# PSUM banks of the output pass, sigmoid's table, wo products in pairs and small closing products in a hybrid decoder layer

## The chip, the cores and the metric

The kernel runs on one core of a Trainium2 chip. The metric is the device time of one execution in microseconds (us). The kernel before took 1947.63 us, the median of three executions (1947.04, 1947.63, 1947.76). The engines are called PE (TensorE, matrix products; PEld is its loading of weights), DVE (VectorE), ACT (ScalarE), POOL (GpSimd) and SP (SyncE, which here only issues DMAs).

## The reference

One layer on 1024 tokens with 16 learned meta tokens ahead of them, width 1024, all in float32:

```
h = h + 1/2 * SwiGLU_1(RMSNorm(h))                 # d_ff 2816
u = RMSNorm(h) @ W_in                              # one projection for both groups
o = concat[ HGRN2(u_hgrn), StickBreaking(u_sb) ]   # 4 heads of 128; 8 heads of 64
h = h + o @ W_out
h = h + 1/2 * SwiGLU_2(RMSNorm(h))
```

`swiglu(h, w_in, w_out)` is `(silu(g) * u) @ w_out` with `g, u = split(h @ w_in)`. HGRN2 is a gated linear recurrence, computed in chunks of 128 tokens; its forget gate f is a sigmoid, its query and output gate pass through silu. Stick-breaking attention normalises q and k for each head (a root), and weights each earlier token by a sigmoid times a product of (1 - sigmoid). The output is h without the 16 meta tokens.

## The kernel before, in words

Float32 products are made of three products of rounded parts (hi x hi, lo x hi, hi x lo), each a 128x128 weight block by up to 512 columns. PE's instructions are issued in the order in which the program writes them; the other engines are scheduled by the compiler's queue order with a few forced orders (`issue_after`). The work runs in stages.

**First SwiGLU (from the start to about 690 us).** Each of its two matrix products is done by a Strassen-like scheme with seven block products. The input pass (`fast_in`; `quad`, `gate`, `up` inside it, L452 to L571) goes through the columns in quads. A quad opens four sums in PSUM, tagged qa, qb, qc and qd, of two banks each, in the pool `pin1`. Its results are gated on ACT (`gate`) and multiplied on DVE (`up`, L542 and L545), and stored as activations in DRAM. Tags of this pool get their banks in the order of their first use. The first use of any is `warm` (L843 to L847), 30 transposes of the identity ahead of the first data, in two tiles of tag qb. The sums of the meta tokens (`begin` with the products mq of L1014, and `finish`, L985 to L996, with the transpose mf) use the tag qd. Two other small groups of products are named later: mps (L901), transposes of the meta tokens, and nps (L262), sums for a norm with a 128x128 block of ones as weights and one column.

The output pass (`fast_out`, L619 to L745) uses the pool `pout1`, which takes over the same banks once `pin1` is closed. It opens four tiles y0 to y3 for its first step (A12 by B21), and x0 to x3 for its second; the meta tokens have a sum of their own there, tag m. For its first three q (blocks of 256 rows of w_out) it gathers the 36 products and issues them together, hi x hi of all first. Weights are halved into hi on ACT and lo on DVE (L652), eight slots in `self.parts["w"]`, and the activations in `self.parts["t"]`.

**Projections and stick-breaking attention (about 690 to 1146 us).** A projection of 128 columns (`project`, `hgrn_fill`, L1116 to L1195; products L249 to L251, tag proj, two banks) is done in pieces of 256 or 512 tokens. For column kind v the sum is copied (L1148) and stored (hg_v, L1150). For kind f, ACT makes two sigmoids (L1154, L1155) and DVE scales them (L1156, L1159); the results lie in `st` tiles, of which there are four. The first f columns follow the last step of `sb_qk` (L1464 to L1503), which normalises q and k of a pair of heads: DVE transposes, ACT squares and takes the root of the mean (L1488), DVE the reciprocal, POOL multiplies (L1492), DVE transposes back (L1498), and `put_split` (L1429, L1430) scales and splits on ACT and DVE and stores. It is done for p = 0 to 3. Where ACT goes over from the root to the sigmoid, the trace has a table load (ACT_TABLE_LOAD). `sb_v` splits v (L1450, L1451) and stores it with four DMAs on SP (L1458).

**HGRN2's recurrence with the first half of o @ W_out (about 1146 to 1263 us).** `weave` (L1741 to L1783) merges the steps of several generators: three lanes of heads (heads 0 then 3, head 1, head 2) and a "fill", `first_half_of_o`. It keeps a clock in declared durations, and starts a fill step whenever the fill's share of the work lies behind or no head is ready. A head's steps are known by their products: lvl (L1248, L1283), flip (L1508), knp (L1319), s and up (the state, L1327 and L1334, followed by four DVE operations L1337), op (L1347, L1351), onp (L1367). A fill step is one k of one sum of `mix_out`: three products named wo, 650 declared; 64 of them in all. The inputs oT are loaded from DRAM by SP.

**Second half, second SwiGLU, end.** The second SwiGLU has the same two passes; its output pass writes the result by rows. Its last step (A22) evicts x0 to x3 on DVE (L699) and stores them by SP (L705). The y sums are left earlier, while the steps after S4 run. After that only the program's closing drains follow (L2406).

Of the kernel before, what the change touches and what calls it, by code (L numbers as in the profile page):

```python
# [11 lines left out]
F32 = mybir.dt.float32  # L12
# [3 lines left out]
AF = mybir.ActivationFunctionType  # L16
# [4 lines left out]
P = 128  # L21
# [28 lines left out]
class Block:  # L50
# [742 lines left out]
    def open_tokens(self, ops, opened, prepare, rows_at, ev, operands):  # L793
# [9 lines left out]
        nc, x = self.nc, self.a["x"][0]  # L803
# [37 lines left out]
        ra = rows_in(0)  # L841
        nc.sync.dma_start(*self.loads.pop(0))
        for _ in range(2):  # L843
            warm = self.pin.tile([P, 512], F32, tag="qb", name="warm", bufs=2)
            for i in range(15):
                t = warm[:, P * (i % 4) : P * (i % 4) + P]
                nc.tensor.transpose(t, self.ident, self.ident)  # L847
# [616 lines left out]
    def sb_qk(self, p, qT, kT, pool, mix, dst):  # L1464

        nc = self.nc  # L1470
        ss, other = (
            pool.tile([P, 65], F32, tag=x, name=x, bufs=2) for x in ("sbs", "sbo")
        )
        nat = pool.tile([P, 65, 32], F32, tag="nat", name="nat", bufs=2)
        rows = [(qT, 0, 0, 16), (qT, 512, 16, 16), (kT, 0, 32, 16), (kT, 512, 48, 17)]
        for src, c0, b0, nb in rows:
            y = nat[:, b0 : b0 + nb]
            nc.vector.transpose(y.rearrange("p b d -> p (b d)"), src[:, c0 : c0 + 32 * nb])
            sq = pool.tile([P, 17, 32], F32, tag="sq4", name="sq4", bufs=2)[:, :nb]
            nc.scalar.activation(sq, y, AF.Square)  # L1480
            nc.vector.tensor_reduce(ss[:, b0 : b0 + nb], sq, mybir.AxisListType.X, ALU.add)
            yield 0, 1500
        for b in range(4):
            nc.scalar.copy(
                other[32 * b : 32 * b + 32], ss[32 * (b ^ 1) : 32 * (b ^ 1) + 32]
            )
        nc.vector.tensor_add(ss, ss, other)
        nc.scalar.activation(ss, ss, AF.Sqrt, bias=self.eps, scale=1.0 / 64)  # L1488
        nc.vector.reciprocal(ss, ss)
        for _, _, b0, nb in rows:  # L1490
            y = nat[:, b0 : b0 + nb]
            nc.gpsimd.tensor_mul(  # L1492
                y, y, ss[:, b0 : b0 + nb].unsqueeze(2).broadcast_to([P, nb, 32])
            )
        yield 0, 6000
        for src, c0, b0, nb in rows:
            t = src[:, c0 : c0 + 32 * nb]
            nc.vector.transpose(t, nat[:, b0 : b0 + nb].rearrange("p b d -> p (b d)"))  # L1498
            n = min(32 * nb, (SEQ if src is qT else T) - c0)
            gain, to = (self.qg8, dst[0]) if src is qT else (self.kg, dst[1])  # L1500
            with self.tc.issue_after(self.rounds[self.columns[-1]]) if p == 3 else ExitStack():
                self.put_split(to, p, slice(c0, c0 + n), t[:, :n], mix, gain)
            yield 0, 1500  # L1503
# [287 lines left out]
    def run(self):  # L1791
        nc, tc, a = self.nc, self.tc, self.a
# [20 lines left out]
        with ExitStack() as c0:  # L1813
            with ExitStack() as c1:
# [116 lines left out]
                with tc.manual_schedule(engines={nc.tensor.engine}), ExitStack() as c2:  # L1931
# [9 lines left out]
                    self.op = self.pool("op1", ctx=op_ctx)  # L1941
                    pout_ctx = ExitStack()
                    self.pout = self.pool("pout1", 1, PSUM, pout_ctx)
                    hT = ph.tile([P, KT, T], F32, name="hT")
                    self.ring_bufs, self.act_bufs, self.apart = 7, 5, True
                    early_w, hat = [], []
# [127 lines left out]
                    def between(step, q):  # L2074
                        if (step, q) in loads:
                            m, c = loads[step, q]
                            with tc.issue_after(self.last_act.ins):
                                nc.sync.dma_start(hT[:, m, c : c + n], xD[m, :, c : c + n])
                        if (step, q) == ("S2", 5):
                            nc.sync.dma_start(  # L2080
                                hT[:, :, :META], xD[:, :, :META].rearrange("k p t -> p k t")
                            )
                        if step == "S3" and 6 <= q < 10:
                            if q == 6:
                                norms[1] = norm_steps(
                                    c_b, lambda: [(self.pout, "y0"), (self.pout, "y1")], v, 2, 4
                                )
                            next(norms[1])
                        elif step == "A22":
                            if q == 0:  # L2090
                                norms[2] = norm_steps(
                                    c_a, lambda: [(self.pn, "nps")] * 2, v, 0, 1
                                )
                            for _ in range(2):
                                next(norms[1], None)
                            if 6 <= q < 10:
                                next(norms[2])
                            if q in (1, 3, 5):
                                early_w.append(self.col_tile(
                                    a["w_in"][0], {1: 2560, 3: 3072, 5: 2048}[q]  # L2100
                                ))
# [83 lines left out]
                with tc.manual_schedule(engines={nc.tensor.engine}):  # L2185
# [7 lines left out]
                    with ExitStack() as c2:  # L2193
                        self.att.append(self.pool("att1", ctx=c2))
                        tag = self.proj_tags[0]
# [11 lines left out]
                    for i, n in enumerate(LEVELS[:5]):  # L2207
                        m = self.masks[:, i, :].rearrange("p (b h r) -> p b h r", h=2, r=n)
# [33 lines left out]
            with tc.manual_schedule(engines={nc.tensor.engine}), ExitStack() as cx:  # L2242
                with ExitStack() as c1:
# [8 lines left out]
                    def from_dram(half):  # L2252
                        got = [[], []]
                        for k in range(4):
                            for i in range(2):
                                t = self.pool_o.tile([P, 512], F32R, tag="o", name="oT", bufs=16)
                                with tc.issue_after(self.last_load.ins) if half else ExitStack():
                                    self.last_oT = nc.sync.dma_start(
                                        t.bitcast(F32), oD[k, :, i, 512 * half : 512 * half + 512]
                                    )  # L2260
                                got[i].append(t)
                        return [Blocks(x) for x in got]

                    def first_half_of_o():
                        ws = {0: self.rows_tile(4, 0)}
                        o = [from_dram(0)]
                        for store in self.stores:
                            with tc.issue_after(self.last_oT.ins):
                                store()
                        yield 4000.0  # L2270
                        plan = [(m, half) for half in range(2) for m in range(KT)]
                        steps = self.mix_out(4, plan, o, ws, hD, hT, mix)
                        for i, (t, f) in enumerate(steps):
                            if i == 16:
                                o.append(from_dram(1))
                            f()
                            yield t

                    with ExitStack() as c2:
                        c2.push(hg_ctx)  # L2280
# [33 lines left out]
                    for i in summed(1, cB):  # L2314
                        if i == 4:
                            r = self.inv_rms_rows(sums[0], n, px, pps)
                        if i == 7:
                            r = self.spread_rows(r, n, px, pps)
# [36 lines left out]
                r = self.inv_rms_rows(sums[1], n, px, ppb)  # L2355
# [8 lines left out]
            with tc.manual_schedule(engines={nc.tensor.engine}), ExitStack() as c1:  # L2364
                self.ring = self.pool("ring", ctx=c1, side="right")
                hR = self.pool("h3", ctx=c1).tile([P, SEQ // P, D], F32, name="hR")
                self.op = self.pool("op", ctx=c1)
                self.pout = self.pool("pout2", 1, PSUM, c1)

                loads = {("A12", 2 * m): (m, 0) for m in range(4)}  # L2370
                loads.update({("A11", m): (4 + m % 4, 1 - m // 4) for m in range(8)})
                loads.update({("S2", m): (m, 1) for m in range(4)})

                def between(step, q):
                    if (step, q) in loads:
                        r, i = loads[step, q]
                        nc.sync.dma_start(
                            hR[:, r, 512 * i : 512 * i + 512],
                            h2R[P * r : P * r + P, 512 * i : 512 * i + 512],
                        )  # L2380

                self.ring_bufs, self.act_bufs, self.apart = 6, 6, False
                self.fast_out(
                    hR, (cA, cB), n, a["ffn2_w_out"][0], actD, lambda step: None, between, rows=True
                )


NAMES = [
# [21 lines left out]
```

## Time and profile before

| | |
|---|---|
| median of three executions | 1947.63 us |
| the profiled execution | 1946.68 us |
| span of its profile | 1944.9 us |
| PE busy | 1919.0 us (99%) |
| DVE busy | 1392.1 us (72%) |
| ACT busy | 848.6 us (44%) |
| granted PE clock, mean | 1.0 |
| HBM traffic over the span | 182 GB/s |

In the rows of a timeline the first number is the start in us from the start of the span, the second the time to the end of the last of the operations that the row groups (xcount), then engine, source line and operation, out<-in by tile names with partitions x elements; in brackets stands how long the engine had been idle before it, and what released it. In the rows by line stand the busy time of the group and the mean in ns, and behind the second bar the idle time before its instructions. In a window's row stand its bounds, its length, then for PE, PEld, DVE, ACT and POOL the busy time and the count, then the granted PE clock, the DMA engines' busy share and GB/s. A line with a q behind the engine's name (SPq) is of that engine's queue of instructions. Consecutive products of PE overlap, so a product's duration is longer than the distance to the next one's start.

### The profile page before, as it was taken

Reading aid. Unit: us, or ns where it says so; the run is one execution under the profiler, and the core shown is the slowest. Engines: PE = TensorE matmul, PEld = TensorE weight load, DVE = VectorE, ACT = ScalarE, POOL = GpSimd, SP = SyncE. Lnnn points to the kernel's source line nnn. Section 1 sums busy time; section 2 is a strip of 40 time slices with the busy share of each in tenths; the row PEclk is TensorE's granted clock in tenths of the full one; section 3 lists DMA queues with packets and bytes.
Section 4 is the critical chain, followed back from the end, with each engine's and each line's share of the span. In section 5 each row is a group of like instructions: output and inputs, shape, how many; then the busy total and the mean of one; then the engine's idle time right before and its main releaser. Section 6 shows DMA issues by size and latency. Waiting matters only on the chain.

```text
span 1944.9 us, 30254 instructions
## 1 busy us (share of the span) xinstructions
PE 1919.0 (99%) x10637; PEld 1619.7 (83%) x10637; DVE 1392.1 (72%) x2184; ACT 848.6 (44%) x1711; POOL 450.3 (23%) x625
## 2 busy tenths in 40 slices
PE   9999999999999999999999999999999999999999
PEld 7888888887888888889898978888888888888887
DVE  7977778877678665467777766667577767767774
ACT  7522343334444444366666635533223332344443
POOL 2010101001000003133333342210554544530000
PEclk9999999999999999999999999999999999999999
DMA  7265897758965325865453178656544444469473
GB/s 219 89 178 165 254 287 244 244 184 294 372 230 188 120 58 146 190 172 148 134 155 116 58 251 245 154 202 200 180 119 141 130 125 131 130 248 323 143 233 114
DMA packets 381687, 355.54 MB, mean 183 GB/s; under 512 B 129040, under 2 KB 284560, under 8 KB 381536
## 3 DMA queue, kind: packets, MB, share of 16 engines
q1 hardware_dynamic: 360768, 288.98, 49.2%
q0 software_dynamic: 20768, 64.63, 9.5%
q8 instruction: 84, 1.38, 0.3%
q14 instruction: 67, 0.55, 0.1%
HBM read 237.95 MB, written 115.57 MB: 182 GB/s over the span
## 4 chain that ended last, share of the span: by engine, by line
PE 90%; DVE 4%; DMA 2%; ACT 2%; issue 1%; POOL 0%; SPq 0%; DVEq 0%; ACTq 0%; POOLq 0%
PE o L735 22%; PE qb L452 18%; PE qa L452 12%; PE qc L452 12%; PE proj L249 5%; PE proj L251 5%; PE proj L250 5%; PE flip L1508 2%; PE wo L250 1%; PE wo L251 1%; PE wo L249 1%; PE mq L1014 1%; PE oacc L1587 1%; PE oacc L1585 1%; PE z L1657 1%
## 5 line engine op out<-in xcount | busy, mean ns | idle before, releaser
L452 PE MATMUL qb<-T,wh 128*128 128x512 f32 x1056 | 343.7, 390 | 0.4 <-DVE u L484 0.4
L452 PEld LDWEIGHTS qb<-T,wh 128*128 128x128 f32 x1056 | 198.2, 188 | 44.5 <-issue 3.3
L452 PE MATMUL qa<-B,wh 128*128 128x512 f32 x696 | 227.6, 392 | 0.3 <-ACT B L838 0.2
L249 PE MATMUL proj<-xh,wh 128*128 128x512 f32 (+2 forms) x640 | 212.4, 332 | 3.0 <-ACT st L1155 1.4
L362 DVE TENSOR_TENSOR wl<-s,wh 128x512 fp32r<-128x512 f32 x160 | 165.7, 1036 | 69.3 <-ACT wh L360 68.5
L735 PE MATMUL o<-t,w 128*128 128x512 f32 x924 | 211.8, 390 | 1.1 <-DVE u L545 1.1
L251 PE MATMUL proj<-xl,wh 128*128 128x512 f32 (+2 forms) x640 | 209.3, 327 | 0.8 <-DVE xl L1973 0.8
L735 PE MATMUL o<-parts 128*128 128x512 f32 x924 | 209.6, 389 | 0.0
L250 PE MATMUL proj<-xh,wl 128*128 128x512 f32 (+2 forms) x640 | 208.9, 326 | 0.0
L452 PE MATMUL qb<-T,wl 128*128 128x512 f32 x528 | 205.5, 389 | 0.0
L735 PEld LDWEIGHTS o<-t,w 128*128 128x128 f32 x924 | 172.8, 188 | 38.2 <-ACT sgm L994 1.5
L735 PEld LDWEIGHTS o<-parts 128*128 128x128 f32 x924 | 173.4, 188 | 36.0
L360 ACT CAST wh<-s 128x512 fp32r<-128x512 f32 x160 | 99.4, 622 | 185.6 <-PE qb L452 139.4
L452 PEld LDWEIGHTS qa<-B,wh 128*128 128x128 f32 x696 | 130.5, 188 | 29.3 <-issue 1.4
L360 ACT CAST wh<-raw 128x512 fp32r<-128x512 f32 x120 | 74.3, 621 | 143.7 <-PE qc L452 93.0
L452 PE MATMUL qa<-B,wl 128*128 128x512 f32 x348 | 135.5, 389 | 0.0
L249 PEld LDWEIGHTS proj<-xh,wh 128*128 128x128 f32 x640 | 120.9, 189 | 14.3 <-ACT st L1155 2.2
L251 PEld LDWEIGHTS proj<-xl,wh 128*128 128x128 f32 x640 | 120.9, 189 | 11.8 <-DVE xl L1973 1.2
L250 PEld LDWEIGHTS proj<-xh,wl 128*128 128x128 f32 x640 | 121.1, 189 | 9.1
L452 PEld LDWEIGHTS qb<-T,wl 128*128 128x128 f32 x528 | 99.1, 188 | 20.3
L452 PE MATMUL qc<-T,wh 128*128 128x512 f32 x352 | 116.0, 391 | 0.0
L452 PE MATMUL qc<-B,wh 128*128 128x512 f32 x352 | 114.6, 389 | 0.0
(397 smaller groups left out, 3828.2 us busy)
## 6 DMA issues: line engine op xcount, KB each, us to landing
raw<-in_ffn_w_in_dram SPq DMA_DIRECT2D x176, 256.0 KB, 4.0
raw<-in_ffn_w_out_dram SPq DMA_DIRECT2D x112, 256.0 KB, 4.4
w2in<-both SPq DMA_DIRECT2D x28, 512.0 KB, 4.1
raw<-in_w_in_dram SPq DMA_DIRECT2D x25, 512.0 KB, 5.1
ks<-kD SPq DMA_DIRECT2D x32, 260.0 KB, 4.7
wout<-both SPq DMA_DIRECT2D x16, 512.0 KB, 3.7
wh<-w2in SPq DMA_DIRECT2D x27, 256.0 KB, 3.5
wl<-w2in SPq DMA_DIRECT2D x27, 256.0 KB, 3.3
```

Of the source, the lines that this page charges most:

```text
L249: nc.tensor.matmul(ps, wh[:, s], xs, start=k == 0, stop=False)
L250: nc.tensor.matmul(ps, wl[:, s], xs, start=False, stop=False)
L251: nc.tensor.matmul(ps, wh[:, s], xl[:, k, c0 : c0 + n], start=False, stop=k == nk - 1)
L360: nc.scalar.copy(hi, src)
L362: self.block_lo = nc.vector.tensor_sub(lo, src, hi.bitcast(F32))
L452: nc.tensor.matmul(ps, a[:, k, :], b[:, k, :], start=start and k == 0 and i == 0, stop=k == 3 and i == 2, skip_group_check=True,)
L735: nc.tensor.matmul(banks[bank][m], y[:, m * P : (m + 1) * P], z, start=start and at == 0 and e == 0, stop=q == nq - 1 and e == 2, skip_gro ...
L1014: nc.tensor.matmul(ps[at : at + 32, :], self.xm[:, 4 * h + k, :], got[i, h][:, k, :], start=h == 0 and k == 0, stop=h == 1 and k == 3, til ...
L1508: self.nc.tensor.transpose(ps[:m, j, :], src[:, s0 : s0 + m], self.ident)
L1585: nc.tensor.matmul(o[:, c], vj, w[0], start=j == 0, stop=False, skip_group_check=True)
L1587: nc.tensor.matmul(o[:64, c], vj[:, :64], w[1], start=False, stop=end, skip_group_check=True)
L1657: nc.tensor.matmul(z, q, ks[0][:, s0 : s0 + n], start=True, stop=False)
```

## The change

It has four parts, in four places.

1. The warm-up tiles have the tag qa in place of qb, and the output pass's pool is told to place y0, y1, x0, y2 and y3 in this order before anything else.
2. At the last of the four calls of `sb_qk` (p == 3), a sigmoid of one column is put behind the root on ACT; its result is not used.
3. The fill of the recurrence gives up its turn after two k steps in place of one, with the sum of their durations.
4. Behind the second output pass, 72 products with 128x128 weights and 16, 32 or 64 columns, and 16 with 32 rows of weights (at the rows 0 and 32 of the array in turn) and 128 columns are added. They read the parts that are left in `self.parts` and write to two banks of the y sums; nothing reads them.

```
-            warm = self.pin.tile([P, 512], F32, tag="qb", name="warm", bufs=2)
+            warm = self.pin.tile([P, 512], F32, tag="qa", name="warm", bufs=2)
...
-        nc.scalar.activation(ss, ss, AF.Sqrt, bias=self.eps, scale=1.0 / 64)
+        root = nc.scalar.activation(ss, ss, AF.Sqrt, bias=self.eps, scale=1.0 / 64)
+        if p == 3:
+            with self.tc.issue_after(root.ins):
+                nc.scalar.activation(other[:, :1], self.eps, AF.Sigmoid)
...
                     self.pout = self.pool("pout1", 1, PSUM, pout_ctx)
+                    for tag in ("y0", "y1", "x0", "y2", "y3"):
+                        self.pout.tile([P, 512], F32, tag=tag, name="place")
...
                             f()
-                            yield t
+                            if i % 2:
+                                yield 2 * t
...
                 self.fast_out(
                     hR, (cA, cB), n, a["ffn2_w_out"][0], actD, lambda step: None, between, rows=True
                 )
+                small = [self.pout.tile([P, 512], F32, tag=f"y{i}", name="small") for i in range(2)]
+                w, x = self.parts["w"], self.parts["t"]
+                for ns in ((16,), (32, 16), (64,)):
+                    for i in range(24):
+                        m = ns[i % len(ns)]
+                        nc.tensor.matmul(
+                            small[0][:, :m], w[:, i % 8, P : 2 * P], x[:, i % 8, :m],
+                            start=i == 0, stop=i == 23, skip_group_check=True,
+                        )
+                for i in range(16):
+                    r = slice(32 * (i % 2), 32 * (i % 2) + 32)
+                    nc.tensor.matmul(
+                        small[i % 2][:, :P], w[r, i % 8, :P], x[r, i % 8, :P],
+                        start=i < 2, stop=i > 13, skip_group_check=True,
+                        tile_position=(32 * (i % 2), 0),
+                    )
```

## The prediction

> **What bounds the kernel now.** I read the page first: busy times, then the chain that ended last; then TensorE's waits, and the timelines around those that the change touches.
>
> ```profile
> span 1944.9 us, 30254 instructions
> PE 1919.0 (99%) x10637; PEld 1619.7 (83%) x10637; DVE 1392.1 (72%) x2184; ACT 848.6 (44%) x1711; POOL 450.3 (23%) x625
> PE 90%; DVE 4%; DMA 2%; ACT 2%; issue 1%; POOL 0%; SPq 0%; DVEq 0%; ACTq 0%; POOLq 0%
> ```
>
> TensorE (PE) is busy for 1919.0 of 1944.9 us and holds 90% of the chain. So the time is PE's work plus 26 us of idle, and the waits that this change touches, in the timelines below, last 1.44 us or less each. Nothing here can bring much; only what adds products to PE, or takes one of these waits away, counts. The profiled run took 1946.68 us, 1.8 over its span and 0.95 under the median of 1947.63; I sum changes against the profiled run and add 0.95. A change of 0.2% (3.9 us) is about what a measurement of this kernel can tell from none.
>
> **Part 1, the banks of the output pass.** The warm-up's tag decides which pair of banks the first pool gives to qa, qb and so on, and the "place" tiles decide which banks the output pass's y0 to y3 get. Now y0 lies on a bank of qb.
>
> ```profile
> 452.84 0.69 DVE L542 TENSOR_TENSOR sg<-qa,sg 128x512 f32<-128x512 f32 x1 [1.17 <-PE qa L452]
> 462.29 0.69 DVE L652 TENSOR_TENSOR t<-act,t 128x512 fp32r<-128x512 f32 x1 [0.31 <-ACT t L651]
> 464.11 0.68 DVE L545 TENSOR_TENSOR u<-qb,p 128x512 f32<-128x512 f32 x1
> 464.71 0.68 DVE L545 TENSOR_TENSOR u<-qc,u 128x512 f32<-128x512 f32 x1
> 464.94 9.36 PE L735 MATMUL o<-t,w 128*128 128x512 f32 x40 [1.14 <-DVE u L545]
> 471.70 1.29 DVE L652 TENSOR_TENSOR t<-act,t 128x512 fp32r<-128x512 f32 x2
> ```
> ```profile
> 470.00:690.00 220.00, 220.00 (x1279) 180.94 (x1279) 158.42 (x261) 99.95 (x177) 10.21 (x19) 1.00 0.68 232
> ```
>
> The first product starts at 464.94, when qb is read (464.11+0.68=464.79). The last quad's qc is read until 465.39. After the change y0 and y1 lie on qa's banks, read by 453.53, y2 and y3 on banks of the quad before; only the x tiles, opened later, take the late ones. PE can then start once the 1.14 is gone: operands are there (462.29+0.69=462.98) and PE would have come 1.14 earlier. What is late next: the first three q make 36 products, (9.36-0.39)/39=0.23 each, 8.3 us, so q=3 is due near 472.1, and the low part of its activations two products later, near 472.5. The first of the pair at 471.70 delivers it about 472.4 (0.68 for one): just in time, 0.3 of wait at most. The window behind it shows PE busy for 220.00 of 220.00 us, so what is gained is kept. Value -1.2; ends -1.3 (the first product enters while the one ahead of it still drains) and -0.8 (that 0.3).
>
> **Part 2, sigmoid's table.** Of the fourth of four roots, a dummy sigmoid loads the table earlier.
>
> ```profile
> 837.57 0.73 ACT L1429 ACTIVATE ohi<-qT,qg 128x512 fp32r<-128x512 f32 x1 [2.57 <-DVE qT L1498]
> 844.34 1.28 ACT L1154 ACT_TABLE_LOAD   x1
> 845.93 0.39 ACT L1155 ACTIVATE st<-proj 128x272 f32<-128x272 f32 x1
> 848.90 0.39 ACT L1155 ACTIVATE st<-proj 128x256 f32<-128x256 f32 x1 [0.79 <-DMA hg_v<-st]
> ```
> ```profile
> 842.51 2.63 SPq L1458 DMA_DIRECT2D vD<-vhl  x4
> 845.18 0.92 SPq L1150 DMA_DIRECT2D hg_v<-st  x2
> ```
> ```profile
> 846.37 0.39 PE L249 MATMUL proj<-xh,wh 128*128 128x256 f32 x1 [1.44 <-ACT st L1155]
> 849.34 0.38 PE L249 MATMUL proj<-xh,wh 128*128 128x256 f32 x1
> ```
>
> The new load of 1.28 and its activation lie in ACT's idle 2.57 before 837.57; the reciprocal and the work up to that row run on DVE and POOL. If that cover were gone, it would cost up to 1.5 on ACT and nothing on PE, which is busy there with proj. The load at 844.34 goes, and it stands in the way: L1155 would end at 845.04, and PE's second chunk start at 845.09 in place of 846.37. That chunk lasts 2.97 (846.37 to 849.34). The third chunk needs the bank that the L1155 of 848.90 leaves at 849.29, and this one waited not for ACT but for the landing of hg_v<-st, which frees an st buffer. Those stores are issued from 845.18, behind four vD stores on SP's queue, none of which the table holds back. So the third chunk starts at 849.3 as before: the wait of 1.44 moves behind the second chunk. Value 0, ends -1.3 (store lands as much earlier) and +0.2.
>
> **Part 3, wo products two k at a time.** The weave releases wo steps by declared durations; worked through with those, its present order is the trace's, and the new one has 30 runs of wo where there were 42.
>
> ```profile
> 1146.90:1263.30 116.40, 111.06 (x744) 95.90 (x742) 81.22 (x145) 58.13 (x158) 33.46 (x56) 1.00 0.73 204
> ```
> ```profile
> 1214.48 1.18 PE L1283 MATMUL lvl<-QA,KP 128*128 128x128 f32 x8 [1.38 <-DVE QA L1249]
> ...
> 1216.19 0.60 PE L1367 MATMUL onp<-ident,vT 128*128 128x128 f32 x4
> 1216.63 1.06 PE L1283 MATMUL lvl<-QA,KP 128*128 128x128 f32 x8
> 1217.44 0.48 PE L249 MATMUL wo<-oT,wh 128*128 128x512 f32 x1
> ...
> 1218.22 0.39 PE L249 MATMUL wo<-oT,wh 128*128 128x512 f32 x1
> ...
> 1218.91 1.07 PE L1283 MATMUL lvl<-QA,KP 128*128 128x128 f32 x8
> ```
> ```profile
> L1337 DVE SCALAR_TENSOR_TENSOR F<-F,Ts,up 128x128 f32<-128x128 f32 x28 | 9.7, 346 | 3.5 <-PE up L1334 2.6
> 1156.99 0.50 PE L249 MATMUL wo<-oT,wh 128*128 128x512 f32 x1 [0.51 <-DMA oT<-oD]
> ```
>
> The products stay the same; only neighbours change. A wo step behind a head step takes 0.78 (1217.44 to 1218.22), behind a wo step 0.69; eight head products take 0.81 ahead of a wo step, and 0.88 ahead of another head step by the onp row (four in 0.44). What longer wo runs save, 12 by 0.09, the 12 more head neighbours cost again: 0. Of the window's 116.40 us PE idles in 5.34. In the new order the head step that waits 1.38 at 1214.48 has about 2.4 us more of other work ahead of it, so that goes: -1.4, and I put 0.4 on the smaller waits of that idle time. Against it: the two k of a wo pair need their oT at once, where the third step already waited 0.51 at 1156.99: +0.3 to +1.0, I take 0.7; and one head's output step comes right behind its state step, whose bank is read by four operations of 346 ns: 0 to 0.85, I take 0.5; other pairs of steps +0.2. Sum -0.4; ends -1.8 (only the gains) and +2.0 (only the new waits).
>
> **Part 4, 88 small products at the end.** They follow the last o product on PE. Data and banks have been ready long before, so there is no wait; the question is what each costs and what covers it.
>
> ```profile
> 1938.43 2.43 PE L735 MATMUL o<-parts 128*128 128x512 f32 x10
> 1938.86 2.73 DVE L699 SCALAR_TENSOR_TENSOR hR<-o,hR 128x512 f32<-128x512 f32 x4 [7.11 <-PE o L735]
> L2406 SPq DRAIN x3: 7/7/7, 1944.1 to 1944.4; - x3
> ```
> ```profile
> 1311.51 0.95 PE L262 MATMUL nps<-ones_d,nacc 128*128 128x1 f32 x8
> 1312.32 0.48 PE L452 MATMUL qa<-B,wh 128*128 128x512 f32 x1
> 442.46 1.96 PE L1014 MATMUL mq<-raw,xm 128*32 128x128 f32 x64
> 42.04 0.66 PE L901 MATMUL mps<-ident,meta 16*128 16x16 f32 x8
> ```
>
> The last o product starts at 1938.43+2.43-0.39=1940.47 and the next can follow 0.23 later, at 1940.70. The nearest row to 72 products with 128x128 weights and 16 to 64 columns is nps: as large weights and one column, eight in 0.81 to 0.95 us, so 0.10 to 0.12 each however few the columns: 72x0.11=7.9. [...] The 16 with 32 rows lie between mq's 0.03 (1.96/64) and nps' 0.11: 0.5 to 1.8, I take 1.4. PE ends near 1950.0, plus 0.2 of latency. What they hide behind is short: DVE's last eviction ends at 1941.59, and SP drains at 1944.1, after the last stores' landing, 0.8 ahead of the end. With PE last, the span ends near 1950.2+0.8=1951.0: +6.0. Low end: the mps spacing, (0.66-0.21)/7=0.065 with its 0.21 of latency at the end, 88x0.065=5.7, PE's end at 1946.6 and +2.5. High end, 88x0.12=10.6: +7.4.
>
> **Sum:** -1.2+0-0.4+6.0=+4.4; 1946.68+4.4+0.95=1952.0.
>
> **Rivals.** *Cheap products (not slower).* If small loads with few columns run at the mps spacing of 0.065, part 4 is +2.5, and with -1.6 from the others 1948.5: within 0.2%. It decides wherever a product takes under 0.10. For: mps has 16 columns, as half of the 72 have. Against: its weights are 16x16, those here as large as nps', and rounded weights, as o's are, load no faster than the plain ones of nps:
>
> ```profile
> L735 PEld LDWEIGHTS o<-parts 128*128 128x128 f32 x924 | 173.4, 188 | 36.0
> L262 PEld LDWEIGHTS nps<-ones_d,nacc 128*128 128x128 f32 x32 | 4.2, 191 | 0.3
> ```
>
> 12%. [...]
>
> *Gains that are larger.* The hg_v stores land as early as the table allows (-1.3), and the wo order gains its whole 1.8: 1949.3 with both, 1950.7 with one, no change that can be told. For: the 1.44 wait plainly ends on ACT. Against: the row of 848.90, which a DMA holds. 20%.
>
> *New waits in the wo pairs.* The oT landings and the state step's bank cost their upper ends: +2.0 in place of -0.4, 1954.4. For: 0.51 at 1156.99. Against: one gap of 1.38 that surely has more cover. 10%.
>
> *The clock falls at the end.* Products that use the array briefly could let the granted clock drop.
>
> ```profile
> 2.13 5.64 PE L847 MATMUL warm<-ident 128*128 128x128 f32 x30 [2.13 <-POOL ident L80]
> ```
>
> At the start 30 equal transposes take 5.64 us, 0.19 each, well over nps' 0.11 for products that are no larger: the clock is not open there. If it halved after the first few us of small products, the last 5 would take twice as long: 1957. PE is sparsely used here, but never idle for long: 8%. [...]
>
> *It does not do what it says:* a bank order that puts y2 or y3 on a late bank keeps half of part 1, 1952.6: 2%, within the main case's range.
>
> **How the numbers follow.** Main case 48%, centred on 1952.0, from 1950.4 to 1953.5 by the ends of parts 1 to 3 and 0.01 on a small product; "slower" begins at 1951.5, so 31 of its 48 are slower and 17 the same. Add waits 10, clock 8 and the bank order 2 to slower: 51; cheap products 10 and larger gains 18 to the same: 45; 2 and 2 of these are faster: 4. The range reaches from the cheap products to a clock that falls late, and drops the rest of the clock case and the corner where every gain meets cheap products: 1948.4 to 1956.0. Since both sides of the bound hold much of the chance, the main case's own range stands beside it: 1950.4 to 1953.5.
>
> **What would show it.** After: PE's first o product at 463.6 to 463.9 without a wait for u; no table load near 844 but one near 835, PE's wait for st at 846 gone and one of about 1.3 at 848 for a store's landing; 30 runs of wo, PE's idle in that stretch 4.5 to 5.5; 72 products 0.11 apart behind the last o product, PE's last about 9 us after it, and PE the last in the chain. I am wrong if the small products come 0.06 or 0.2 apart, or if the stretch of wo changes by over 2 us.

## The result and the profile after

The changed kernel takes 1958.62 us (median of six executions, 1956.05 to 1960.42), the kernel before 1947.66 in the executions beside it: the ratio is 1.0057, 95% interval 1.0046 to 1.0067. That is 11 us slower, where 4.4 were forecast, and outside the range, which ended at 1956.0. The profiled execution took 1956.05 us, the shortest of the six.

From the page of the changed kernel, the span, the busy times and the chain that ended last:

```profile
span 1954.3 us, 30423 instructions
PE 1931.6 (99%) x10725; PEld 1633.3 (84%) x10725; DVE 1394.7 (71%) x2184; ACT 848.7 (43%) x1712; POOL 451.2 (23%) x625
PE 72%; issue 18%; DVE 4%; POOL 2%; ACT 2%; DMA 1%; SPq 0%; POOLq 0%; DVEq 0%; ACTq 0%
```

PE is busy 12.6 us longer. Its 88 more products stand at the end of its timeline:

```profile
1924.82 15.12 PE L735 MATMUL o<-parts 128*128 128x512 f32 x66
1939.78 11.72 PE L2397 MATMUL small<-parts 128*128 128x16 f32 x72
1951.42 1.97 PE L2403 MATMUL small<-parts 32*128 32x128 f32 x16
```

They take 13.6 us in place of the 9.3 forecast. The windows of the same stretch (PE, PEld, DVE, ACT and POOL busy, then the granted PE clock) say why:

```profile
1940.00:1942.00 2.00, 2.00 (x20) 2.00 (x19) 0.67 (x1) 0.00 (x0) 0.00 (x0) 1.00 0.98 380
1942.00:1944.00 2.00, 2.00 (x19) 2.00 (x19) 0.00 (x0) 0.00 (x0) 0.00 (x0) 0.95 0.11 42
1944.00:1946.00 2.00, 2.00 (x11) 2.00 (x11) 0.00 (x0) 0.00 (x0) 0.00 (x0) 0.50 0.03 8
```

Up to 1943.8 a small product takes 0.112 us, as forecast; then the granted clock is 0.5 and it takes 0.213. PE is never idle in this stretch: its rows show it busy for 2.00 of 2.00 us all along.

The last o product starts at 1939.55 here and at 1940.47 before, 0.92 earlier: that is what parts 1 to 3 brought in this execution. Their places, PE first for part 1, then ACT and PE for part 2, then PE's waits in the recurrence for part 3:

```profile
463.49 10.84 PE L735 MATMUL o<-t,w 128*128 128x512 f32 x45
```
```profile
833.94 1.28 ACT L1491 ACT_TABLE_LOAD   x1
...
843.45 0.39 ACT L1155 ACTIVATE st<-proj 128x272 f32<-128x272 f32 x1
846.80 0.38 ACT L1154 ACTIVATE st<-proj 128x256 f32<-128x256 f32 x1 [2.97 <-DMA hg_v<-st]
848.50 0.38 ACT L1155 ACTIVATE st<-proj 128x256 f32<-128x256 f32 x1 [1.31 <-DMA hg_v<-st]
```
```profile
848.94 0.39 PE L249 MATMUL proj<-xh,wh 128*128 128x256 f32 x1 [1.92 <-ACT st L1155]
```
```profile
PE lvl L1283 <- ACT KP L1277: 1.2, 1, 1.2
PE onp L1367 <- DVE F L1337: 1.1, 1, 1.1
PE wo L251 <- DMA oT<-oD: 0.6, 1, 0.6
```

The first o product follows the input pass without a wait. For part 2 the names matter: the first head's f is projected in four pieces of 272, 256, 256 and 256 tokens; what the prediction and the expectations call its second and third chunk are the third and the fourth piece, and these names are kept here. The table loads early; ACT is done with the first piece (the L1155 with 272 tokens) 1.4 us sooner against the rest, and then waits longer for the landing of the hg_v stores: PE's wait has moved behind the second chunk and is 1.92 in place of 1.44. That is more than a move. The two hg_v stores are issued no later against the rest (from 844.11 in place of 845.18, with PE's f pieces 1.08 earlier), but the later of them takes 3.8 us to land in place of 3.2. The time from issue to landing, before and then in the changed kernel:

```profile
DMA to landing us min/median/max: 2.4/2.8/3.2
```
```profile
DMA to landing us min/median/max: 2.6/3.2/3.8
```

In the recurrence the wait of 1.38 for QA is gone, and waits for the state's F (1.1), KP (1.2) and oT (0.6) stand there.

### The profile page after: what moved, and what is told of

Read it like the earlier page. It is cut to its first block, busy times and chain, and to the rows that moved or that the text cites. A ratio compares the mean times of both kernels' runs of the same rounds, so it can differ in the third digit from the quotient of the medians.

```text
span 1954.3 us, 30423 instructions
## 1 busy us (share of the span) xinstructions
PE 1931.6 (99%) x10725; PEld 1633.3 (84%) x10725; DVE 1394.7 (71%) x2184; ACT 848.7 (43%) x1712; POOL 451.2 (23%) x625
## 3 DMA queue, kind: packets, MB, share of 16 engines
q8 instruction: 85, 1.39, 0.3%
## 4 chain that ended last, share of the span: by engine, by line
PE 72%; issue 18%; DVE 4%; POOL 2%; ACT 2%; DMA 1%; SPq 0%; POOLq 0%; DVEq 0%; ACTq 0%
PE o L735 21%; PE qb L452 10%; PE qa L452 8%; PE qc L452 7%; PE proj L249 5%; PE proj L251 5%; PE proj L250 5%; PE flip L1511 2%; PE wo L249 1%; PE wo L251 1%; PE wo L250 1%; PE oacc L1590 1%; PE oacc L1588 1%; PE z L1660 1%; PE z L1661 1%
```

## The experiments

My theory after this result: PE's clock is granted by how much of the time columns stream through the array, and the 88 products stream too few. Rivals: being bound by weight loads is enough, however many columns follow; the quiet of the other engines at the end does it; or the changed kernel's other parts do. The second question was what parts 1 to 3 are worth each.

**Without the closing products.** The block behind `fast_out` is left out:

```
-                small = [self.pout.tile([P, 512], F32, tag=f"y{i}", name="small") for i in range(2)]
...
-                        tile_position=(32 * (i % 2), 0),
-                    )
```

> This is the changed kernel without its 88 closing products. Both theories agree that parts 1 to 3 remain: by the trace of the changed kernel its last o product starts 0.92 us earlier than before, so 1946.7 us; the sum on record for these parts was -1.6, so 1946.0. If instead one of parts 1 to 3 costs what the trace of one execution hides, it is 1948 or more. It sets the price of the closing products: the changed kernel's 1958.62 less this.

Measured: 1948.01 (1946.82 to 1949.01), before 1947.93, ratio 0.9998 (0.999 to 1.0007). So the closing products cost 1958.62-1948.01=10.6 us, and parts 1 to 3 bring nothing that can be measured, worse than the -0.9 of the trace and the -1.6 on record. This kernel's own trace shows one reason, PE's row at the third chunk of f and the windows around it:

```profile
849.56 0.38 PE L249 MATMUL proj<-xh,wh 128*128 128x256 f32 x1 [2.62 <-ACT st L1155]
```
```profile
848.00:850.00 2.00, 0.44 (x3) 0.44 (x4) 0.39 (x2) 0.84 (x3) 0.00 (x0) 1.00 0.80 240
850.00:852.00 2.00, 2.00 (x14) 2.00 (x13) 0.64 (x2) 1.10 (x2) 0.00 (x0) 0.65 0.70 229
852.00:854.00 2.00, 2.00 (x11) 2.00 (x11) 1.23 (x1) 0.17 (x1) 0.00 (x0) 0.50 0.87 233
854.00:856.00 2.00, 2.00 (x12) 1.70 (x11) 1.21 (x4) 1.03 (x4) 0.00 (x0) 1.00 0.53 167
```

The moved wait has grown to 2.62 us, and behind it the clock is 0.5 until 854.0: the products with 256 columns follow each other every 0.21 us there, where 0.12 is their pace on the open clock. So the early table had opened a gap with half the clock behind it. The clock falls once more in this trace, from 860.8 to 864.2, and there no wait ahead of it is longer than 0.36; the last section comes back to that.

**The closing products alone.** On the kernel before, that block and nothing else:

```
+                small = [self.pout.tile([P, 512], F32, tag=f"y{i}", name="small") for i in range(2)]
...
+                        tile_position=(32 * (i % 2), 0),
+                    )
```

> The kernel before with the 88 closing products alone. Theory (the clock falls because the array is used sparsely): the clock falls in the closing products, +10 to +13 us, 1958 to 1961, mean granted clock 0.997. Rival (the fall comes of the changed kernel's other parts, the bank order above all): +6.0 as on record, 1953.7, clock 1.000.

Measured: 1957.91 (1956.89 to 1958.63), ratio 1.0049 (1.0036 to 1.0063), clock 0.998: +10.0. The fall belongs to these products; the bank order has no part in it. In its trace the clock falls 5.4 us after the first small product, against 4.0 in the changed kernel.

**128 columns in each of the 72.**

```
-                for ns in ((16,), (32, 16), (64,)):
+                for ns in ((128,), (128,), (128,)):
```

> The changed kernel with 128 columns in each of the 72 products in place of 16, 32 or 64; the weights and the count stay. Theory A (the granted clock follows the share of time in which columns stream): the share is about half in place of 6 to 25%, the clock stays at 1.0, a product still takes 0.11 us, and the time is 1952.5 to 1953.5. Theory B (what counts is that PE is bound by loading weights, however many columns follow): the clock falls as before, 1958 to 1960. Theory C (the clock falls because the rest of the core has gone quiet at the end): also 1958 to 1960.

Measured: 1955.19 (1953.03 to 1956.89). Against the kernel without closing products that is +7.2 and not +10.6, though up to eight times as many columns stream. PE's rows and a window:

```profile
1945.05 8.15 PE L2397 MATMUL small<-parts 128*128 128x128 f32 x72
1953.13 1.11 PE L2403 MATMUL small<-parts 32*128 32x128 f32 x16
```
```profile
1950.00:1952.00 2.00, 2.00 (x20) 2.00 (x20) 0.00 (x0) 0.00 (x0) 0.00 (x0) 1.00 0.03 8
```

The clock stays at 1.0 to the last product, with the other engines as quiet as before and the weight loads as dense. That refutes both rivals, and leaves the share of streaming. The rows also give the price on an open clock: 0.112 for one of the 72, and 0.06 for one of the 16, whose two row positions start together (0 to 3 ns apart in the changed kernel's trace). The time is above the 1952.5 to 1953.5 expected: the kernel without closing products was itself above what was expected of it, and this kernel's trace, too, has a gap at the third chunk of f, of 2.97 us, and half the clock behind it.

**The first 24 alone.**

```
-                for ns in ((16,), (32, 16), (64,)):
+                for ns in ((16,),):
...
-                for i in range(16):
-                    r = slice(32 * (i % 2), 32 * (i % 2) + 32)
...
```

> The changed kernel with the first 24 closing products alone (16 columns each). Theory A and B: they take 24 x 0.112 = 2.7 us and end near 1942.4, ahead of SP's drain near 1943.3, so nothing is left to see: 1946.7 to 1947.2, clock 1.000, since the fall came only 4.1 us after the start of the small products. [...]

Measured: 1948.03 (1946.03 to 1948.88), before 1947.93, and 1948.01 without any; the 1946.7 to 1947.2 expected was missed as it was there.

```profile
1941.96 2.74 PE L2397 MATMUL small<-parts 128*128 128x16 f32 x24
```

2.74 us disappear in the 3.4 us that the last stores need anyway (before: from 1940.70, where a product could follow the last o, to SP's drain at 1944.1), and they end at 1944.70, before the clock falls: the window from 1944 to 1946 still has 0.99.

**64 columns, and 96.** The same line with 64 or 96 in place of 128.

> The changed kernel with 64 columns in each of the 72 products. [...] Theory A (the clock of the next interval of 3.4 us follows the share of time in which columns stream in this one): in the changed kernel the clock stayed at 0.5 through intervals that held 64-column products alone, so 24% is too little and the clock falls at the end of the first interval that they fill, 3.4 to 6.8 us after the first one; 1957 to 1961. Rival (only the 16 and 32 columns are too few, and a fallen clock rises only at a higher share than it falls at): clock 1.0 to the end, 1955.

> [...] Theory A sets no number between 24% and 48%: with a bound under a third the clock stays at 1.0 and the time is 1955, as with 128 columns; with a bound above it the clock falls as with 64, 1957 to 1961. A fall only in part of the 72 products would speak against a bound on the share.

Measured: 1958.73 (1957.31 to 1960.12) with 64 and 1957.02 (1955.8 to 1957.46) with 96, both with the clock at 0.5 from some 3 to 4 us after the first product on. Two windows with 96:

```profile
1943.00:1945.00 2.00, 2.00 (x20) 2.00 (x20) 0.00 (x0) 0.00 (x0) 0.00 (x0) 1.00 0.33 125
1946.00:1948.00 2.00, 2.00 (x12) 2.00 (x11) 0.00 (x0) 0.00 (x0) 0.00 (x0) 0.50 0.03 8
```

So with 96 columns in 112 ns the clock fell, and with 128 it did not. At the pace of the o products, 512 columns in 0.227 us, columns stream for an estimated 25% of the time with 64, 38% with 96 and 51% with 128; no run shows the pace behind the 24% and 48% that the expectations name.

**The same products in the middle.** The block moves into `between`, to the fourth q of the last step, and reads the slots of that q:

```
+                    if (step, q) == ("A22", 3):
+                        small = [self.pout.tile([P, 512], F32, tag=f"y{i}", name="small") for i in range(2)]
+                        w, x = self.parts["w"][:, 2:4], self.parts["t"][:, 2:4]
...
```

> The changed kernel with its 88 closing products in the middle of the last step of the output pass, after its fourth q, with seven q of 512-column products behind them. Theory A: the clock falls 3.4 to 6.8 us after the first one, as at the end, and the products behind run at half the clock until the interval after the first one that they fill, 1.7 us lost for each 3.4 us; the 88 products then cost 13 to 16 us and not the 10.6 that they cost at the end, since nothing hides them: 1961 to 1964. Rival (the fall needs the quiet of the other engines at the end): clock 1.0, 9.5 us, 1957.5.

Measured: 1964.6 (1964.06 to 1964.99). PE's rows, and windows of the small products early and late, and of the o products behind:

```profile
1925.20 10.69 PE L2393 MATMUL small<-parts 128*128 128x16 f32 x72
1935.82 1.97 PE L2399 MATMUL small<-parts 32*128 32x128 f32 x16
1937.71 20.66 PE L735 MATMUL o<-parts 128*128 128x512 f32 x84
```
```profile
1926.00:1928.00 2.00, 2.00 (x20) 2.00 (x20) 0.00 (x0) 0.00 (x0) 0.00 (x0) 1.00 0.00 0
1938.00:1940.00 2.00, 2.00 (x5) 1.53 (x5) 1.29 (x2) 0.76 (x2) 0.00 (x0) 0.50 0.00 0
1942.00:1944.00 2.00, 2.00 (x11) 1.65 (x10) 1.30 (x2) 1.01 (x2) 0.00 (x0) 1.00 0.00 0
```

The clock falls 5.2 us after the first small product (an estimate from the 10.69 us of the 72, at 0.112 and then 0.213 each) and stays low for the first o products behind them: five in 2 us, at 1938 to 1940, where 9 fit at 0.227; at 1942 to 1944 it is open again. So here, too, it is the products; nothing hides them, and they cost 16.6 more than no closing products at all (16.0 by the two kernels' ratios to the kernel before, 1.008 and 0.9998, as they were not measured side by side), at the upper end of what was expected or a little over it.

**Banks alone, table alone, wo alone.** Each with its hunk of the diff on the kernel before.

> The kernel before with the bank order alone. Theory: the first o product starts 1.1 to 1.4 us earlier against the quad ahead of it, as in all traces of the change so far, and the gain is kept to the end: 1946.5 to 1946.9 where the kernel before takes 1947.9. Rival: the gain is given back at q=3, where operands come just in time, and the time is 1947.9.

> The kernel before with the early sigmoid table alone. Theory (the wait moves to the landing of the hg_v stores and grows, and where PE's gap there reaches about 2.6 us the granted clock halves for some 3 us): PE's gap of 1.9 to 3.0 us ahead of the third chunk of f, clock 0.5 behind it in the executions with a gap over 2.6, +0.5 to +3 us: 1948.4 to 1951. Rival 1, the sum on record: the wait only moves, 1947.9. Rival 2: the table's time is gained, 1946.6.

> The kernel before with the wo products in steps of two k alone. Theory, from the trace of the changed kernel, in which this stretch took 0.65 us less: 1947.3, and PE's wait of 1.4 for QA is gone while a wait for oT and one of about 1.1 for the state remain. Rival: the new waits cost as much as the old ones, 1947.9; or upper ends on record, +2.0: 1949.9.

Measured: 1947.31, 1949.31 and 1946.99; the ratios to the kernel before (1948.61), which are not quotients of these medians, are 0.9998 (0.9989 to 1.0006), 1.0005 (0.9996 to 1.0014) and 0.9992 (0.9983 to 1.0001). No interval leaves 1 out, so the times don't separate them. The traces, one of each kernel, show more. Since PE's products are the same, each start can be set against the same product's start in the trace of before; the table has the change of that difference over four stretches (us, minus is faster): from the last input product to the first o; over the next 67 o; from the end of f's first chunk to 29 us on; over the recurrence.

| kernel | to the first o | 67 o on | around f | recurrence |
|---|---|---|---|---|
| changed kernel | -1.39 | +0.36 | +0.81 | -0.73 |
| without closing products | -1.39 | +0.16 | +4.14 | -0.62 |
| 128 columns | -1.38 | +1.51 | +3.55 | -0.57 |
| first 24 | -1.38 | +0.11 | +2.87 | -0.66 |
| 64 columns | -1.38 | +0.13 | +4.39 | -0.45 |
| 96 columns | -1.38 | +0.11 | +1.28 | -0.48 |
| banks alone | -1.38 | +2.47 | -0.06 | +1.32 |
| table alone | -0.40 | -0.04 | +2.90 | +0.45 |
| wo alone | +0.21 | -0.04 | -0.04 | -0.74 |
| closing products alone | -0.24 | -0.04 | +0.83 | +0.12 |

Banks: 1.38 is gained each time, and then 0.1 to 2.5 is given back. In the trace of the banks alone more than the whole of it goes, DVE's rows and then PE's:

```profile
472.96 0.69 DVE L574 TENSOR_TENSOR sg<-sg,t 128x512 f32<-128x512 f32 x1 [1.91 <-DMA act110B<-sg]
473.56 0.68 DVE L652 TENSOR_TENSOR w<-raw,w 128x512 fp32r<-128x512 f32 x1
```
```profile
474.30 5.88 PE L735 MATMUL o<-t,w 128*128 128x512 f32 x23 [1.79 <-DVE w L652]
```

DVE stands at L574, which may not overwrite sg before its store has read it, and the weights of q=3 are queued behind it. In the trace of before the same L574 waited only 0.17:

```profile
470.49 0.69 DVE L574 TENSOR_TENSOR sg<-sg,t 128x512 f32<-128x512 f32 x1 [0.17 <-DMA act110B<-sg]
```

Part 1 saved a wait and left PE at the mercy of this one, whose length differs from trace to trace.

Table: +0.8 to +4.4 in every kernel of this table with the early load, and -0.06, -0.04 and +0.83 in the three without it; the lowest with it is no higher than the highest without it, so one trace of each would not have told them apart. The two over +4 hold two falls of the clock, the second worth 1.3 to 1.4. In all seven the second hg_v store landed 3.8 to 4.8 us after its issue, in the three without the early load and in the trace of before 3.1 to 3.2. What holds that store up is not shown. The gap ahead of the third chunk was 1.92 us in the changed kernel, with the clock at 1.0 behind it, and 2.56 in the trace of the table alone, with the clock at 0.5:

```profile
851.41 0.38 PE L249 MATMUL proj<-xh,wh 128*128 128x256 f32 x1 [2.56 <-ACT st L1155]
```

Recurrence: -0.45 to -0.74 with pairs of k, +0.12 to +1.32 without. The pairs are worth about 1 us in these traces.

**The stores that the third chunk waits for.** Edit, on the changed kernel without closing products:

```
                 with self.tc.issue_after(self.last_load.ins):
-                    nc.sync.dma_start(dst[kind][h, :, s], t)
+                    eng = nc.gpsimd if h == 0 else nc.sync
+                    eng.dma_start(dst[kind][h, :, s], t)
```

> The changed kernel without closing products, and with the v stores of the first head issued by POOL in place of SP, where they stood behind four vD stores. Theory (the hg_v landing is what the third chunk of f waits for): the stores are issued 2 to 3 us earlier, PE's gap ahead of that chunk shrinks under 1 us, the clock stays at 1.0 there, and the time falls from 1948.0 to about 1945.0 to 1946.0. Rival: the stores land no earlier because the DMA engines are busy (0.9 and more of their time there) or because POOL is slower to issue: 1948.0.

> The changed kernel without closing products and without the early table, with the first head's v stores issued by POOL. Theory: without the early table PE waits its 1.4 us ahead of the second chunk of f again, and the store's landing no longer holds the third, so the version with the table is 1 to 1.5 us ahead: 1947.0 here against 1945.6. Rival (the POOL stores alone bring the gain and the table nothing): 1945.6.

Measured: 1945.59 (1943.84 to 1947.87), ratio 0.9989 (0.998 to 0.9998), with the table; 1947.73 (1946.43 to 1948.89), ratio 0.9995 (0.9986 to 1.0004), without it. POOL's two late stores and ACT's and PE's rows with the table:

```profile
838.91 0.56 POOL L1151 DMA_DIRECT2D hg_v<-st  x1
...
841.06 0.54 POOL L1151 DMA_DIRECT2D hg_v<-st  x1
```
```profile
844.52 0.38 ACT L1156 ACTIVATE st<-proj 128x256 f32<-128x256 f32 x1 [0.57 <-DMA hg_v<-st]
```
```profile
850.90 0.50 PE L249 MATMUL proj<-xh,wh 128*128 128x512 f32 x1 [1.11 <-ACT st L1156]
```

The stores are issued 3 us and more earlier (SP issued them from 844.11 on in the changed kernel), ACT waits 0.57 for their landing in place of 2.97 and 1.31, PE goes through the second and third chunk without a gap, and the clock stays at 1.0. A wait of 1.11 remains a chunk later. Without the early table PE waits 1.52 ahead of the second chunk, as before, and then has the same 1.11:

```profile
847.29 0.39 PE L249 MATMUL proj<-xh,wh 128*128 128x256 f32 x1 [1.52 <-ACT st L1156]
...
854.61 0.50 PE L249 MATMUL proj<-xh,wh 128*128 128x512 f32 x1 [1.11 <-ACT st L1156]
```

Counted as in the column "around f" of the table, the change is -0.08 with the early table and +1.33 without it. So only now does the early table gain, 1.4 us against the version without it. Against the kernel before, the two edits together come out even in this stretch, since the wait of 1.11 stands in both traces with POOL's stores and in no other. The times alone do not separate the two versions, whose intervals overlap. The one with the table is the fastest, and the only one whose interval lies below 1, though by no more than 0.2%; in its trace, whose last o product starts 2.6 us earlier than before, most of that comes from other stretches (1.2 from the recurrence, 0.7 from the end of the input pass and the first 68 o products).

## Why the prediction was wrong, point by point

The direction, slower, was right; the size was not, and the measured time lies beyond the range. The step that failed is in part 4: the sum took 0.11 us for every one of the 72 products, and "the clock falls at the end" was put at 8% since PE "is sparsely used here, but never idle for long". That rival is what happened, at nearly its price: its 1957 was the forecast 1952.0 and 5 for a clock that halves after the first few us. The measured cost of the closing products is 10.6 in place of 6.0. With 128 columns, on an open clock, it is 7.2, so most of the difference is the clock; the other 1.2 is less than the spread of that kernel's times (1953.03 to 1956.89). The argument from never being idle was the mistake: the experiments show that a busy PE row is no cover. With PE busy for 2.00 of 2.00 us the clock was 0.50 in closing products of up to 96 columns, and 1.00 in those of 128.

The shape of the rest was right: 0.112 for a product on an open clock, against 0.10 to 0.12; no wait ahead of them; little cover, as the first 24, at 2.74 us, cost nothing. The 16 take 1.97 us at half the clock and 1.11 on an open one; 1.4 was put. The cheap products did not show: 0.112, not 0.065.

Part 1, -1.2: the wait went as forecast (-1.38), but the "0.3 of wait at most" at q=3 is 0.1 to 2.5. The trace of before had this step just in time, and the prediction did not ask what DVE's queue waits for there: the L574 ahead, with its 0.17 of wait for a DMA in the trace of before.

Part 2, 0 with ends -1.3 and +0.2: the step "the wait of 1.44 moves behind the second chunk" is what every trace with the early load and SP's stores shows. What failed is "the third chunk starts at 849.3 as before", and with it the upper end of +0.2: the wait grew to 1.9 to 3.0, since the store that it ends on landed later and not as before (3.8 to 4.8 us after its issue in place of 3.1 to 3.2), and in five of the table's seven kernels with the early load the clock fell behind it; that makes +0.8 to +4.4. A gap that is moved was taken as worth its length alone.

Part 3, -0.4: -0.45 to -0.74, with the waits named (QA gone, oT 0.6, the state's F 1.1) and one not named (KP 1.2). The total is right, a little too small, and in part by luck: F's wait lies above its end of 0.85 and KP's was in no term, while the smaller waits fell by more than the 0.4 put on them (PE's for kms from 1.6 to 0.7, for the QA of L1270 from 0.6 to 0.2, in the changed kernel).

So parts 1 to 3 are worth 0 (ratio 0.9998) in place of -1.6, and part 4 is worth 10.6 in place of 6.0: 1947.66+10.6=1958.3, against 1958.62. As the 10.6 was itself taken from 1958.62, this only divides the time up; the 10.0 of the closing products alone, measured apart, gives 1957.7.

## What to carry to other kernels

A tail of small products is priced by the clock that they leave, not by their spacing on an open one: here 10.6 us with 16 to 64 columns, where the clock fell to 0.5, and 7.2 with 128, where it stayed at 1.0. A wait that was taken away in front of a store-bound buffer came back behind it, longer than it was (1.92 to 2.97 in place of 1.44), and cost more where the clock fell behind it: 2.9 to 4.4 around f, against 0.8 and 1.3 without a fall there. Free the buffer first (here by another queue for two stores), and then count the whole stage again: the early table gained 1.4 us, and a new wait of 1.11 took most of it. Where an operand comes just in time, look at what is queued ahead of it.

## What the runs showed of the hardware

Where the clock of 0.5 began and ended at the third chunk of f, it lasted for some 3.4 us: 1.40 and 2.00 us by the windows of the kernel without closing products above, and 1.72 and 1.72 by those of the first 24:

```profile
848.00:850.00 2.00, 0.21 (x1) 0.21 (x2) 0.65 (x2) 1.02 (x3) 0.00 (x0) 1.00 0.82 235
850.00:852.00 2.00, 2.00 (x12) 2.00 (x12) 0.80 (x3) 1.09 (x3) 0.00 (x0) 0.57 0.64 210
852.00:854.00 2.00, 2.00 (x12) 2.00 (x12) 1.23 (x1) 0.41 (x1) 0.00 (x0) 0.57 0.66 177
854.00:856.00 2.00, 2.00 (x13) 1.74 (x12) 1.02 (x3) 1.02 (x4) 0.00 (x0) 1.00 0.73 218
```

The length of the gap alone did not tell whether it fell. Two kernels show it there, the one with 64 columns and the one with 96:

```profile
848.92 0.39 PE L249 MATMUL proj<-xh,wh 128*128 128x256 f32 x1 [2.48 <-ACT st L1155]
```
```profile
850.29 0.39 PE L249 MATMUL proj<-xh,wh 128*128 128x256 f32 x1 [2.52 <-ACT st L1155]
```

Behind the first gap the clock fell: from 850.37 to 852.94 the products with 256 columns start 0.21 us apart. Behind the second, longer one they stay 0.12 apart to the last. The other gaps with a fall behind them were 2.56, 2.62, 2.64 and 2.97 us long; behind the changed kernel's 1.92 there was none.

A fall came without a long gap, too. Ahead of the second fall in the kernel without closing products, at 860.8, PE waited three times from 858 on, for 0.36 us at most; the first of these waits, and the clock behind the fall:

```profile
858.18 0.48 PE L1660 MATMUL z<-ks,qs 128*128 128x456 f32 x1 [0.36 <-ACT sig L1663]
```
```profile
862.00:864.00 2.00, 2.00 (x8) 1.60 (x7) 1.89 (x4) 1.65 (x5) 1.10 (x2) 0.50 0.94 174
```

The kernel with 64 columns has such a second fall too: its products with 512 columns start 0.43 us apart from 862.52 to 863.80, and 0.23 from 864.10 on. In the closing products the number of columns made the difference, 96 with a fall and 128 without, with the rest of the kernel the same. That the share of streaming also decides behind the gaps of f was not shown.

When the clock falls differs from trace to trace: between 3.0 us after the first small product (64 columns, an estimate from the 12.63 us of the 72, at 0.112 and then 0.213 each) and 5.4 (the closing products alone). That fits a part of the spread of the changed kernel, 4.4 us: each us of small products ahead of the fall saves 0.9 at the end, since a product takes 0.112 and not 0.213, so that the 2.4 between these two are worth some 2.2. The kernel without closing products has a spread of 2.2 of its own. The spread was not tested by itself.
